# Neighbourhood attention: the channel sums of q and k squares as one fp32 matmul, or as an upper and a lower part in two passes

## The chip, the cores and the metric

The kernel runs on one core of one Trainium2 chip. The metric is device time in microseconds (us) of one execution. The engines of the core are TensorE (PE in the profile, its weight loads PEld), VectorE (DVE), ScalarE (ACT), GpSimd (POOL) and SyncE (SP, which here only issues transfers). Each engine works through its own list of instructions in a fixed order and waits on semaphores for the others.

## The reference, cut to what matters

A two-layer trunk: layer 0 is an mLSTM and Hyena mixer, layer 1 is a 2-D neighbourhood attention; each is followed by a squared-ReLU MLP. The change lies in layer 1, in the normalisation of q and k:

```python
def odd_mixer(hx, hc, w_qkv, qn, kn, rpb, w_out, ctx_out):
    def project(h):
        p = (h @ w_qkv).reshape(b_, l_, 3, NA_HEADS, NA_HD)       # 16 heads of 64 channels
        q = rms_norm(p[:, :, 0], qn) * NA_HD ** -0.5               # x * rsqrt(mean(x*x) + EPS) * gain
        k = rms_norm(p[:, :, 1], kn)
        v = p[:, :, 2]
    ...
```

There are 1024 latent tokens and 256 context tokens, 1024 channels, all in float32.

## The kernel before, in words

Activations lie with channels on the 128 partitions and tokens along the free dimension, in three groups of tokens: two of 512 latent tokens and one of 256 context tokens (`GR`). Products of weights and activations are made from split operands: a float32 value is held as an upper part, rounded to the type fp32r, and a lower part, the remainder in fp32r (`split`, lines 110 to 113: ACT copies, which rounds, and DVE subtracts). A projection (`gemm`, lines 170 to 180) issues three fp32r matmuls for each of 8 blocks of channels: 24 matmuls for one group.

The attention layer goes over 8 pairs of heads. For each pair, `natten_proj` makes q, k and v. It works group by group: two groups of q (q0, q1), three of k (k0, k1, k2) and three of v (v0, v1, v2). Each q or k group goes through `normed`: ACT squares the projection out of PSUM (L900), PE sums the squares over the 64 channels of each head by a matmul with a block matrix of ones, `bd` (L902), ACT takes the mean, the logarithm and the exponential (L904 to L906), and DVE refines the reciprocal root and applies it (L907 to L913). ACT then rounds the result into `Q` or `Kt` (L932, L938) and DVE makes the lower parts (helper line L96). So five calls of `normed` stand in each pair, 40 in all: 32 of 512 tokens and 8 of 256. Both operands of L902 are plain float32; each such matmul shows in the trace as two PE records.

`natten_attn` then treats four column blocks of the grid (`cb`), each for the two heads of the pair (`hh`): scores (PE, L978 and L979), row maximum and bias (DVE, L982 to L986), exponentials (ACT, L989 and L990), division (DVE, L994), transposes of the probabilities (PE, L999 and L1006), copies of them to SBUF (ACT L1001 into tiles of the tag `s2`; DVE L1008), and the product with v (PE, L1014 and L1018). After the last pair the output projection follows.

Nothing in the source fixes the order in which the two functions of neighbouring pairs interleave. A scheduler lays the instructions of each engine out before the run, by priorities and by when it thinks that operands and buffers are free. The attention is written under `pr("na")`, a raised priority of 500; `natten_proj` under `pr("np")`, which has none. Buffers are part of it. PSUM holds three banks for projections (`g`), three for scores and outputs (`f`), one for transposes (`m`) and one for the sums of squares (`n`): `PS3` in line 63. In SBUF, `s2()` and `n2()` are two sets of four buffers of 128x512 each (lines 86 to 90). Before the change, a call of `normed` takes three `n2` buffers (`sq`, which later serves as `v`, then `y` and `r`), and no `s2` buffer; the transposed probabilities of a column block take four `s2` buffers.

Of the kernel before, what the change touches and what calls it, by code (L numbers as in the profile page):

```python
# [9 lines left out]
F32 = mybir.dt.float32  # L10
F32R = mybir.dt.float32r
AF = mybir.ActivationFunctionType
ALU = mybir.AluOpType
# [4 lines left out]
P = 128  # L18
# [9 lines left out]
def kernel(ctx: ExitStack, tc: tile.TileContext, A, out):  # L28
    nc = tc.nc
    V, S, T, G = nc.vector, nc.scalar, nc.tensor, nc.gpsimd  # L30
    cnt = [0]

    base = ctx.enter_context(tc.tile_pool(name="base", bufs=1))
# [5 lines left out]
    def mk(pool, shape, tag, bufs, dt=F32):  # L39
        cnt[0] += 1  # L40
        return pool.tile(shape, dt, tag=tag, bufs=bufs, name=f"{tag}_{cnt[0]}")
# [18 lines left out]
    def pr(k):  # L60
        k = HP.get(k, k)
        return ExitStack() if k is None else tc.high_priority(k)
# [13 lines left out]
    def pt(shape, tag):  # L76
        cnt[0] += 1
        return psp[0].tile(shape, F32, tag=tag, bufs=psp[1][tag], name=f"ps{tag}_{cnt[0]}")
# [7 lines left out]
    def s2(shape=None):  # L86
        return mk(base, shape or [P, 512], "s2", 4)

    def n2(shape=None):
        return mk(base, shape or [P, 512], "n2", 4)  # L90
# [4 lines left out]
    def tt(o, a, b, op, e=None):  # L95
        return (e or V).tensor_tensor(out=o, in0=a, in1=b, op=op)  # L96
# [4 lines left out]
    def sub(o, a, b):  # L101
        return tt(o, a, b, ALU.subtract)

    def mul(o, a, b):
        return tt(o, a, b, ALU.mult)

    def stt(o, a, s, b, op0, op1):
        return V.scalar_tensor_tensor(out=o, in0=a, scalar=s, in1=b, op0=op0, op1=op1)  # L108
# [41 lines left out]
    def wload(at, src, e=None, ks=(0, 8), into=None):  # L150
        with pr(at):
            wp_ = wpool[0]
            raw = mk(wp_, [P, 8, P], "wr", 1)
            r = slice(*ks)
            nc.sync.dma_start(raw[:, r], src)
            if into is None:
                hi = mk(wp_, [P, 8, P], "wh", 2, F32R)
                lo = mk(wp_, [P, 8, P], "wl", 2, F32R)
            else:
                hi, lo = [mk(into[0], [P, 8 * P], t, into[2], F32R).rearrange("p (k c) -> p k c", c=P) for t in into[1]]  # L160
            split(hi[:, r], lo[:, r], raw[:, r], e)
        for f in msteps[:MS]:
            f()
        del msteps[:MS]
        return hi, lo
# [4 lines left out]
    def gemm(w, h, g, n, M=P, ks=range(8), tag="g"):  # L170

        hi, lo = w
        hh, hl = h
        ps = pt([P, 512], tag)
        ks = list(ks)
        for i, k in enumerate(ks):
            T.matmul(ps[:M, :n], hi[:, k, :M], hh[g][:, k, :n], start=(i == 0), stop=False)  # L177
            T.matmul(ps[:M, :n], hi[:, k, :M], hl[g][:, k, :n], start=False, stop=False)  # L178
            T.matmul(ps[:M, :n], lo[:, k, :M], hh[g][:, k, :n], start=False, stop=(i == len(ks) - 1))  # L179
        return ps  # L180
# [697 lines left out]
    KC0 = (0, 8, 24, 32)  # L878

    def natten_consts(pool):  # L880
        bd = mk(pool, [P, P], "bd", 1)
        nc.scalar.dma_start(bd, A["bdones"])
        qk = mk(pool, [P, 2], "qkn", 1)
        nc.scalar.dma_start(qk, A["qkn"])
        gain = mk(pool, [P, 1], "gain", 1)
        stt(gain, qk[:, 0:1], 0.125, qk[:, 1:2], ALU.mult, ALU.mult)
        return bd, gain

    def natten_proj(hp, h, ap_, nl, cst, order=((0, 0), (0, 1), (1, 0), (1, 1), (1, 2), (2, 0), (2, 1), (2, 2))):

        with pr("np"):
            bd, gain = cst

            Q = [mk(nl, [P, LAT], "Q", 4, F32R) for _ in range(2)]
            Ql = [mk(nl, [P, LAT], "Ql", 3, F32R) for _ in range(2)]
            for hh in range(2):
                G.memset(Ql[hh][64 - 64 * hh:128 - 64 * hh].bitcast(F32), 0.0)
            def normed(ps, n, sc):
                sq = n2()
                S.activation(sq[:, :n], ps[:, :n], AF.Square)  # L900
                p2 = pt([P, 512], PN)
                T.matmul(p2[:, :n], bd, sq[:, :n], start=True, stop=True)  # L902
                v, y, r = sq, n2(), n2()
                S.activation(v[:, :n], p2[:, :n], AF.Identity, bias=epsc, scale=1.0 / 64)  # L904
                S.activation(y[:, :n], v[:, :n], AF.Ln)
                S.activation(y[:, :n], y[:, :n], AF.Exp, scale=-0.5)  # L906
                mul(r[:, :n], y[:, :n], y[:, :n])  # L907
                stt(v[:, :n], r[:, :n], -0.5, v[:, :n], ALU.mult, ALU.mult)
                stt(r[:, :n], v[:, :n], 1.5, y[:, :n], ALU.add, ALU.mult)
                if sc is None:  # L910
                    mul(r[:, :n], ps[:, :n], r[:, :n])
                else:
                    stt(r[:, :n], ps[:, :n], sc, r[:, :n], ALU.mult, ALU.mult)  # L913
                return r

            Kt = [mk(ap_, [P, NT], "KK", 4, F32R) for _ in range(2)]
            vT = mk(nl, [P, NT], "vT", 2)
            w = {}
            for j, g in order:
                t0, n = GR[g]  # L920
                if j not in w:
                    w[j] = wload("qkv" if hp else "q0", A["w_qkv"][3 * hp + j], E4 if hp == 0 else None, into=(nl, ("Q", "Q"), 4) if hp == 0 and j == WQ else None)
                ts = slice(t0, t0 + n)
                ps = gemm(w[j], h, g, n)
                if j == 0:
                    r = normed(ps, n, gain)
                    blkd = lambda x: x.rearrange("p (c r q) -> p c r q", c=4, q=16)
                    rv = r.rearrange("p (r c q) -> p c r q", c=4, q=16)
                    for hh in range(2):
                        a = slice(64 * hh, 64 * hh + 64)  # L930
                        for b in (0, 64):
                            S.copy(blkd(Q[hh][b:b + 64, ts]), rv[a])  # L932
                        sub(blkd(Ql[hh][a, ts]), rv[a], blkd(Q[hh][a, ts]).bitcast(F32))
                elif j == 1:
                    r = normed(ps, n, None)
                    for hh in range(2):
                        a, b = slice(64 * hh, 64 * hh + 64), slice(64 - 64 * hh, 128 - 64 * hh)
                        S.copy(Kt[hh][a, ts], r[a, :n])  # L938
                        sub(Kt[hh][b, ts], r[a, :n], Kt[hh][a, ts].bitcast(F32))
                else:  # L940
                    with pr("v0" if hp == 0 else None):
                        S.copy(vT[:, ts], ps[:, :n])
            return Q, Ql, Kt, vT
# [169 lines left out]
    with tc.tile_pool(name="gp", bufs=1, reuse_waits="tile", side="right") as gp:  # L1113
        cst = mlstm_consts(gp)
        with tc.tile_pool(name="ml", bufs=1, reuse_waits="tile") as ml:
# [35 lines left out]
            for d in range(FM[2], 8):  # L1151
                out1(d)
    gkc.close()
    cst = natten_consts(ctx.enter_context(tc.tile_pool(name="cn", bufs=1, side="right")))
    with tc.tile_pool(name="xg", bufs=1, reuse_waits="tile", side="right") as xp:
        xg = [mk(xp, [P, 8, n], f"x{g}", 1) for g, (t0, n) in enumerate(GR)]
# [5 lines left out]
        for g, (t0, n) in enumerate(GR):  # L1162
            for d in range(8):
                hi, lo = [x[:, 2 * (d % 4):2 * (d % 4) + 2] for x in w2[d // 4]]
# [53 lines left out]
    with tc.tile_pool(name="xg1", bufs=1, reuse_waits="tile", side="right") as xp:  # L1218
# [3 lines left out]
        hi, lo = wload("ow2", A["w_o"][:, :, 7].rearrange("d p c -> p d c"), E1)  # L1222
# [145 lines left out]
```

## Time and profile before

| | |
|---|---|
| median of 3 runs | 3346.32 us (3345.22 to 3348.22) |
| the profiled execution: time, span | 3341.84 us, 3340.1 us |
| PE busy in the span | 3232.4 us (97%) |
| DVE, ACT, POOL busy | 2056.8 (62%), 1200.4 (36%), 96.5 us (3%) |
| mean granted TensorE clock | 0.991 |
| first and last matmul with `bd` (L902) start | 1916.9 and 2482.1 us |

Busy times are summed from records, and matmul records overlap their neighbours, so the step from one matmul's start to the next says more than a record's length. "idle before, releaser" in a row names what ended an engine's wait. The lines that carry the argument are shown in the prediction.

### The profile page before, as it was taken

Reading aid. Unit: us, or ns where it says so; the run is one execution under the profiler, and the core shown is the slowest. Engines: PE = TensorE matmul, PEld = TensorE weight load, DVE = VectorE, ACT = ScalarE, POOL = GpSimd, SP = SyncE. Lnnn points to the kernel's source line nnn. Section 1 sums busy time; section 2 is a strip of 40 time slices with the busy share of each in tenths; the row PEclk is TensorE's granted clock in tenths of the full one; section 3 lists DMA queues with packets and bytes.
Section 4 is the critical chain, followed back from the end, with each engine's and each line's share of the span. In section 5 each row is a group of like instructions: output and inputs, shape, how many; then the busy total and the mean of one; then the engine's idle time right before and its main releaser. Section 6 shows DMA issues by size and latency. Waiting matters only on the chain.

```text
span 3340.1 us, 45203 instructions
## 1 busy us (share of the span) xinstructions
PE 3232.4 (97%) x18044; PEld 2637.5 (79%) x18044; DVE 2056.8 (62%) x3790; ACT 1200.4 (36%) x2539; POOL 96.5 (3%) x160
## 2 busy tenths in 40 slices
PE   7799999999999999999999999999999999999999
PEld 4678887778877888888888777777777788888887
DVE  4958997556684444544445877666666754455454
ACT  5742221343442212111121576666664422121111
POOL 0000000000000000000000011111110000000000
PEclk9899999999999999999999999999999999999999
DMA  6432224776522212121111221222234111111111
GB/s 208 163 110 67 81 73 146 231 241 208 189 97 95 70 57 89 57 89 64 51 45 32 79 69 59 70 64 70 67 96 144 65 62 46 49 51 47 48 45 70
DMA packets 140876, 306.11 MB, mean 92 GB/s; under 512 B 12497, under 2 KB 74057, under 8 KB 139258
## 3 DMA queue, kind: packets, MB, share of 16 engines
q1 hardware_dynamic: 131018, 266.60, 24.5%
q0 software_dynamic: 6464, 28.84, 2.8%
q10 hardware_dynamic: 3184, 7.78, 0.7%
q8 instruction: 142, 2.33, 0.3%
q14 instruction: 68, 0.56, 0.1%
HBM read 255.93 MB, written 43.05 MB: 90 GB/s over the span
## 4 chain that ended last, share of the span: by engine, by line
PE 77%; DVE 8%; DMA 3%; ACT 2%; issue 1%; SPq 0%; ACTq 0%; DVEq 0%
PE psg L177 13%; PE psg L178 13%; PE psg L179 13%; PE psf L313 8%; PE psf L312 8%; PE psf L314 8%; DMA wm<-in_w_mod 3%; PE psf L1014 2%; PE psm L999 1%; DVE b L96 1%; PE psf L978 1%; PE psf L979 1%; DVE n L108 1%; DVE q L96 1%; PE psf L1018 1%; PE psm L218 1%
## 5 line engine op out<-in xcount | busy, mean ns | idle before, releaser
L177 PE MATMUL psg<-h,wh 128*128 128x512 f32 (+1 forms) x2728 | 1014.8, 372 | 13.5 <-ACT h L289 7.1
L179 PE MATMUL psg<-h,wl 128*128 128x512 f32 (+1 forms) x2728 | 1003.9, 368 | 5.7 <-DVE wl L113 5.4
L178 PE MATMUL psg<-h,wh 128*128 128x512 f32 (+1 forms) x2728 | 1007.9, 370 | 1.0 <-DVE h L108 0.9
L177 PEld LDWEIGHTS psg<-h,wh 128*128 128x128 f32 x2728 | 516.5, 189 | 109.4 <-issue 17.3
L179 PEld LDWEIGHTS psg<-h,wl 128*128 128x128 f32 x2728 | 516.2, 189 | 93.4 <-DVE wl L113 10.6
L178 PEld LDWEIGHTS psg<-h,wh 128*128 128x128 f32 x2728 | 516.3, 189 | 91.7 <-issue 14.2
L108 DVE SCALAR_TENSOR_TENSOR x<-psf,modT,x 128x512 f32<-128x512 f32 (+1 forms) x512 | 347.1, 683 | 218.8 <-PE psf L314 218.7
L313 PE MATMUL psf<-al,w2h 128*128 128x512 f32 (+1 forms) x1280 | 471.6, 369 | 0.6 <-DVE al L113 0.6
L314 PE MATMUL psf<-ah,w2l 128*128 128x512 f32 (+1 forms) x1280 | 470.9, 368 | 0.0
L312 PE MATMUL psf<-ah,w2h 128*128 128x512 f32 (+1 forms) x1280 | 468.6, 369 | 0.1
L112 ACT CAST w2h<-w2r 128x1024 fp32r<-128x1024 f32 x64 | 67.3, 1051 | 765.9 <-PE psf L313 595.9
L113 DVE TENSOR_TENSOR wl<-wr,wh 128x1024 fp32r<-128x1024 f32 (+2 forms) x144 | 172.9, 1200 | 213.3 <-ACT wh L112 212.7
L312 PEld LDWEIGHTS psf<-ah,w2h 128*128 128x128 f32 x1280 | 240.4, 188 | 44.4 <-ACT ah L112 2.6
L313 PEld LDWEIGHTS psf<-al,w2h 128*128 128x128 f32 x1280 | 241.2, 189 | 43.3 <-DVE al L113 2.3
L314 PEld LDWEIGHTS psf<-ah,w2l 128*128 128x128 f32 x1280 | 241.2, 188 | 40.4 <-issue 0.5
L112 ACT CAST wh<-wr 128x1024 fp32r<-128x1024 f32 (+2 forms) x144 | 148.4, 1031 | 249.2 <-PE psg L178 207.6
L108 DVE SCALAR_TENSOR_TENSOR rr<-psg,rr 128x512 f32<-128x512 f32 x160 | 101.3, 633 | 176.6 <-ACT rr L301 176.6
L113 DVE TENSOR_TENSOR w2l<-w2r,w2h 128x1024 fp32r<-128x1024 f32 x64 | 78.2, 1222 | 151.6 <-ACT w2h L112 149.9
L301 ACT ACTIVATE rr<-psg 128x512 f32<-128x512 f32 x160 | 88.0, 550 | 194.7 <-PE psg L179 193.3
L113 DVE TENSOR_TENSOR al<-rr,ah 128x512 fp32r<-128x512 f32 x160 | 101.8, 636 | 84.1 <-ACT ah L112 84.1
L112 ACT CAST ah<-rr 128x512 fp32r<-128x512 f32 x160 | 92.4, 578 | 170.0 <-DVE rr L108 170.0
L108 DVE SCALAR_TENSOR_TENSOR h<-psf,modT,h 128x512 f32<-128x512 f32 x128 | 94.2, 747 | 44.2 <-PE psf L314 44.2
(286 smaller groups left out, 4046.2 us busy)
## 6 DMA issues: line engine op xcount, KB each, us to landing
wm<-in_w_mod SPq DMA_DIRECT2D x96, 512.0 KB
wr<-in_w SPq DMA_DIRECT2D x64, 512.0 KB
w2r<-in_w SPq DMA_DIRECT2D x64, 512.0 KB
big<-d SPq DMA_DIRECT2D x39, 640.0 KB
TM<-in_rpbT POOLq DMA_DIRECT2D x64, 384.0 KB, 3.4
wr<-in_w_in SPq DMA_DIRECT2D x29, 512.0 KB
wr<-in_w_qkv SPq DMA_DIRECT2D x24, 512.0 KB
d<-b SPq DMA_DIRECT2D x8, 1280.0 KB
```

The costliest lines, as they stand in the source:

```text
L96: return (e or V).tensor_tensor(out=o, in0=a, in1=b, op=op)
L108: return V.scalar_tensor_tensor(out=o, in0=a, scalar=s, in1=b, op0=op0, op1=op1)
L112: S.copy(hi, x)
L113: (e or V).tensor_tensor(out=lo, in0=x, in1=hi.bitcast(F32), op=ALU.subtract)
L177: T.matmul(ps[:M, :n], hi[:, k, :M], hh[g][:, k, :n], start=(i == 0), stop=False)
L178: T.matmul(ps[:M, :n], hi[:, k, :M], hl[g][:, k, :n], start=False, stop=False)
L179: T.matmul(ps[:M, :n], lo[:, k, :M], hh[g][:, k, :n], start=False, stop=(i == len(ks) - 1))
L301: S.activation(r[:, :n], ps[:, :n], AF.Relu)
L312: T.matmul(ps[:, :n], w2h[:, d], ah[g], start=(i == 0), stop=False)
L313: T.matmul(ps[:, :n], w2h[:, d], al[g], start=False, stop=False)
L314: T.matmul(ps[:, :n], w2l[:, d], ah[g], start=False, stop=(i == 1))
L1014: T.matmul(po[64 * hh:64 * hh + 64, rb], Vw[:, rb + j, 64 * hh:64 * hh + 64], pT[hh][0][rb][:, j], start=(j == 0), stop=False)
```

## The change

`bd` is kept as fp32r; it is loaded into a plain tile first and copied by ACT. The squares are split into an upper part (`hi`, a fourth `n2` buffer) and a lower part (`lo`, an `s2` buffer), and L902 becomes two fp32r matmuls into the same PSUM bank.

```diff
     def natten_consts(pool):
-        bd = mk(pool, [P, P], "bd", 1)
-        nc.scalar.dma_start(bd, A["bdones"])
+        bd, raw = mk(pool, [P, P], "bd", 1, F32R), s2([P, P])
+        nc.scalar.dma_start(raw, A["bdones"])
+        S.copy(bd, raw)
...
             def normed(ps, n, sc):
-                sq = n2()
+                sq, hi = n2(), mk(base, [P, 512], "n2", 4, F32R)
                 S.activation(sq[:, :n], ps[:, :n], AF.Square)
+                S.copy(hi[:, :n], sq[:, :n])
+                lo = mk(base, [P, 512], "s2", 4, F32R)
+                tt(lo[:, :n], sq[:, :n], hi[:, :n].bitcast(F32), ALU.subtract)
                 p2 = pt([P, 512], PN)
-                T.matmul(p2[:, :n], bd, sq[:, :n], start=True, stop=True)
+                T.matmul(p2[:, :n], bd, hi[:, :n], start=True, stop=False)
+                T.matmul(p2[:, :n], bd, lo[:, :n], start=False, stop=True)
                 v, y, r = sq, n2(), n2()
```

The scheduler also lays out the whole attention layer anew. Lines of the changed kernel behind L902 are five higher: L904 becomes L909, L999 becomes L1004, and so on; the copy to `hi` is L902 there, and the two matmuls are L906 (upper part) and L907 (lower part).

The first place is PE, in the attention of the second pair of heads. Before, the matmul with `bd` for a group of the next pair (`psn`) stands between scores (`psf`), transposes (`psm`) and projections (`psg`):

```order
L954 MATMUL psm_18103<-ident,vs_18101 128x128 x4
L978 MATMUL psf_18167<-KK_17530,Q_17524 128x384
L979 MATMUL psf_18167<-KK_17530,Ql_17526 128x384
L902 MATMUL psn_18441<-n_3270_18439,bd_8340 128x512
L999 MATMUL psm_18138<-ident,pe_18119 128x128 x3
L178 MATMUL psg_18464<-h_1651_8778,wh_18460 128x512
L179 MATMUL psg_18464<-h_1650_8777,wl_18461 128x512
L177 MATMUL psg_18464<-h_1650_8777,wh_18460 128x512
```

Now the transposes of the last column block follow on one another with no projection between them:

```order
L984 MATMUL psf_18371<-KK_17582,Ql_17578 128x384
L1004 MATMUL psm_18342<-ident,pe_18323 128x128 x3
L1004 MATMUL psm_18348<-ident,pe_18329 128x128 x3
L1019 MATMUL psf_18408<-s_3265_18346,Vw_18312 64x128
L1011 MATMUL psm_18354<-ident,pe_18323 128x128 x2
L1011 MATMUL psm_18354<-ident,pe_18329 128x128 x2
L1004 MATMUL psm_18389<-ident,pe_18370 128x128 x3
L1004 MATMUL psm_18395<-ident,pe_18376 128x128 x3
```

and the lower part for q0 of the next pair stands directly behind the last of these transposes:

```order
L1023 MATMUL psf_18408<-pc_18359,Vc_17922 64x128
L1011 MATMUL psm_18401<-ident,pe_18370 128x128 x2
L1011 MATMUL psm_18401<-ident,pe_18376 128x128 x2
L907 MATMUL psn_18478<-s_3298_18476,bd_8340 128x512
L1023 MATMUL psf_18408<-pc_18406,Vc_17922 64x128
```

Its upper part (L906 into the same `psn_18478`) stands 149 rows further up, in the middle of the attention. Between the two, projections of two more groups are found, q1 and k0; the last of their matmuls stands 50 rows ahead of L907. With q0 they fill the three `g` banks.

The second place is ACT, at the start of the second of the five calls. Before, the work of the attention (`pe`, `s`, `o`, `Vw`) stands between the steps of a call:

```order
L904 ACTIVATE n_3270_18439<-psn_18441,epsc 128x512
L905 ACTIVATE n_3272_18443<-n_3270_18439 128x512
L906 ACTIVATE n_3272_18443<-n_3272_18443 128x512
L1001 COPY s_3216_18189<-psm_18185 128x384
L1001 COPY s_3218_18195<-psm_18191 128x384
L900 ACTIVATE n_3278_18489<-psg_18464 128x512
L989 ACTIVATE pe_18246,st_18240<-pe_18246,st_18240 128x384
L1192 COPY o_18225<-psf_18204 128x256
L990 ACTIVATE pe_18246,st_18240<-psf_18239,st_18240 128x256
```

Now the calls of one pair stand behind one another, and the first step of a call (L909) behind the four roundings (L937) of the call ahead of it:

```order
L909 ACTIVATE n_3296_18472<-psn_18478,epsc 128x512
L910 ACTIVATE n_3300_18481<-n_3296_18472 128x512
L911 ACTIVATE n_3300_18481<-n_3300_18481 128x512
L901 ACTIVATE n_3303_18521<-psg_18496 128x512
L1197 COPY o_18429<-psf_18408 128x256
L902 CAST n_3304_18522<-n_3303_18521 128x512
L937 CAST Q_18432<-n_3301_18482 64x512 x2
L937 CAST Q_18433<-n_3301_18482 64x512 x2
L909 ACTIVATE n_3303_18521<-psn_18527,epsc 128x512
```

The pattern repeats for pairs 2 to 7. SP's transfers keep their order; on POOL two neighbours change places in each pair. Outside the attention layer only the load and copy of `bd` move, near 895 us.

## The prediction

> **What bounds the kernel now.** I read the table of engines first, then the table of stretches over the attention layer, cut where the scores of a new pair of heads begin (1947.5, 2015.3, 2094.1 us).
>
> ```profile
> PE 3232.4 (97%) x18044; PEld 2637.5 (79%) x18044; DVE 2056.8 (62%) x3790; ACT 1200.4 (36%) x2539; POOL 96.5 (3%) x160
> ```
> ```profile
> core 0: us, PE busy (x) PEld busy (x) DVE busy (x) ACT busy (x) POOL busy (x), PEclk, DMA share, GB/s
> 1947.50:2015.30 67.80, 63.67 (x444) 49.22 (x444) 50.24 (x121) 48.81 (x123) 10.32 (x16) 1.00 0.23 71
> 2015.30:2094.10 78.80, 78.40 (x528) 61.78 (x528) 54.47 (x123) 51.59 (x129) 11.91 (x18) 1.00 0.22 68
> ```
>
> One pair takes 78.8 us, and PE works 78.4 of them. DVE has 54.5 us of work in it and ACT 51.6, so neither limits, provided that the projection of the next pair always lies beside the attention of this one. The first pair (67.8 us) already leaves PE idle for 4.1 us.
>
> **What the change saves on PE.** The chain of work shows what the two fp32 passes hold PE for, and the timeline of PE what an fp32r matmul holds it for (step from start to start):
>
> ```profile
> 2069.49 0.86 PE psn L902 x2
> ```
> ```profile
> 1949.46 0.39 PE L177 MATMUL psg<-h,wh 128*128 128x512 f32 x1
> 1949.69 0.39 PE L178 MATMUL psg<-h,wh 128*128 128x512 f32 x1
> ...
> 2496.74 0.28 PE L177 MATMUL psg<-h,wh 128*128 128x256 f32 x1
> 2496.86 0.28 PE L178 MATMUL psg<-h,wh 128*128 128x256 f32 x1
> ```
>
> A call of 512 tokens holds PE for 0.86 us, and afterwards for 2 x 0.23 (1949.69 - 1949.46) = 0.46: 0.40 saved. For 256 tokens half of 0.86 is 0.43, and 2 x 0.12 = 0.24 stay: 0.19. Over 32 and 8 calls this is 12.8 + 1.5 = 14.3 us, 4 x 0.40 + 0.19 = 1.8 per pair.
>
> **What it adds.** Each call gains a rounding on ACT and a subtraction on DVE ahead of its matmul. The MLP's split has both in the same shape:
>
> ```profile
> L113 DVE TENSOR_TENSOR al<-rr,ah 128x512 fp32r<-128x512 f32 x160 | 101.8, 636 | 84.1 <-ACT ah L112 84.1
> L112 ACT CAST ah<-rr 128x512 fp32r<-128x512 f32 x160 | 92.4, 578 | 170.0 <-DVE rr L108 170.0
> ```
>
> That is 4.5 x 0.58 = 2.6 us of ACT and 4.5 x 0.64 = 2.9 us of DVE per pair. By busy time alone the 78.8 us would cover both. But the order of the instructions is new, and two things in it take the cover away. The lower part lives in an `s2` buffer; all four of these go to the attention's probabilities first, so the lower part of q0 waits until the attention of the running pair is through. Meanwhile q0, q1 and k0 hold the three `g` banks, and PE has no projection to put between the last column blocks. And as a call now takes all four `n2` buffers, the calls follow one another, on ACT literally: the first step of q1 stands behind the roundings of q0's result.
>
> **Term 1, the projection as a chain.** Durations from the groups of one pair (2039.2 to 2118.1 us), shapes kept apart:
>
> ```profile
> L904 ACT ACTIVATE n<-psn,epsc 128x512 f32<-128x512 f32 x4 | 2.8, 690 | 1.3 <-PE psn L902 1.3
> L905 ACT ACTIVATE n<-n 128x512 f32<-128x512 f32 x4 | 2.6, 638 | 0.1
> L906 ACT ACTIVATE n<-n 128x512 f32<-128x512 f32 x4 | 2.5, 632 | 0.1
> L96 DVE TENSOR_TENSOR n<-n 128x512 f32<-128x512 f32 x4 | 2.8, 689 | 0.0
> L108 DVE SCALAR_TENSOR_TENSOR n<-n,n 128x512 f32<-128x512 f32 x8 | 5.5, 692 | 0.3
> L108 DVE SCALAR_TENSOR_TENSOR n<-psg,gain,n 128x512 f32<-128x512 f32 x2 | 1.5, 748 | 0.0
> L932 ACT CAST Q<-n 64x512 fp32r<-64x512 f32 x8 | 4.9, 618 | 0.1
> L938 ACT CAST KK<-n 64x512 fp32r<-64x512 f32 x4 | 2.5, 612 | 0.0
> L112 ACT CAST wh<-wr 128x1024 fp32r<-128x1024 f32 x3 | 3.1, 1047 | 3.5 <-PE psg L178 3.5
> L108 DVE SCALAR_TENSOR_TENSOR n<-n,n 128x256 f32<-128x256 f32 x2 | 0.9, 426 | 0.1
> ```
>
> From the first ACT step of q0 to that of q1: 0.69 + 0.64 + 0.63 on ACT, 0.69 + 2 x 0.69 + 0.75 on DVE, 4 x 0.62 on ACT: 7.25 us. q1 to k0 the same. k0 to k1 has two roundings instead of four, and the rounding of a weight block (1.05) inside: 7.0. k1 to k2: 5.95. k2, at 256 tokens 0.426 / 0.692 of that, and the lower part of k: 4.1. Sum 31.6, and some twenty handovers of 0.03 us: 32.2 us from the lower part of q0 to the next pair's scores, which need all five. PE has in this time, by the new order, 62 projection matmuls of 512 tokens (62 x 0.23 = 14.3) and 24 of 256 (2.9), the second half of an output (1.7) and nine passes of `bd` (1.9): 20.8. So PE stands idle for 11.4 us per pair. No row shows such a chain without cover; the bounds are 8 us (if extra steps found their place while the matmuls run) and 15 us (if each handover via PE costs another 0.5).
>
> **Term 2, the end of the attention without cover.** The first pair before has a piece of just this order. Transposes of a column block's two heads begin:
>
> ```profile
> 1955.94 0.49 PE L999 MATMUL psm<-ident,pe 128*128 128x128 f32 x3
> ...
> 1961.58 0.52 PE L999 MATMUL psm<-ident,pe 128*128 128x128 f32 x3
> ...
> 1970.07 0.49 PE L999 MATMUL psm<-ident,pe 128*128 128x128 f32 x3
> ...
> 1985.32 0.52 PE L999 MATMUL psm<-ident,pe 128*128 128x128 f32 x3
> ...
> 1990.32 0.52 PE L999 MATMUL psm<-ident,pe 128*128 128x128 f32 x3 [0.46 <-DVE pe L994]
> ...
> 1992.70 0.66 PE L1006 MATMUL psm<-ident,pe 128*128 128x128 f32 x4
> ...
> 1998.66 0.44 PE L978 MATMUL psf<-KK,Q 128*128 128x384 f32 x1 [1.27 <-ACT pe L990]
> ...
> 2000.85 0.52 PE L999 MATMUL psm<-ident,pe 128*128 128x128 f32 x3 [0.57 <-DVE pe L994]
> ```
>
> From 1990.32 to 2000.85 the rows of PE are those of the new order, and 10.5 us pass; the wait of 1.27 is for a score bank that the exponentials hold. From one head's transposes to the other's, 5.0 us (1985.32 to 1990.32); from these to the end of the last transposes 2.8 (1992.70 + 0.4). The uncovered end thus takes 10.5 + 5.0 + 2.8 = 18.3 us. PE's work of attention per pair is 78.4 less 144 x 0.23 + 48 x 0.12 for projections and 3.9 for L902, 35.6 us, 8.9 per column block; by the counts of rows the end holds 1.15 of one, 10.2. Idle: 8.1 us; bounds 5 and 10. The earlier blocks keep somewhat fewer projections between their steps: 1 us more.
>
> **The sum per pair.** PE's work 78.4 - 1.8 = 76.6, plus 11.4 + 8.1 + 1.0 idle: 97.1, against 78.8: +18.3. Six pairs (the second to the seventh) go so: +110 us.
>
> The first pair has nearly no projection from its second block on. From its scores (1947.5) to the first transposes 8.4 us, to the second head's 5.6, three times from second head to first (8.5 at 1961.58, 10.5 at 1990.32; I take 9.6), twice 5.0, the end 7.8, the chain 32.2: 92.8 against 67.8: +25. Its own projection, ahead of its scores, becomes such a chain as well: L904 of q0 starts at 1918.4, the scores at 1947.5, 29.1 us later. The chain needs 32.2 and two copies of v (0.9) that stand in it, and starts 0.6 later: +4.6. The last pair has other work beside it, in the old order: 0.
>
> The load of `bd`: ACT waits in its place before, too, and longer than a load and a copy:
>
> ```profile
> 905.72 0.62 ACT L112 CAST h<-big 128x512 fp32r<-128x512 f32 x1 [3.67 <-DVE big L108]
> ```
>
> Cost 0 to 1 us, taken as 0, while that idle time lasts. Total: 110 + 25 + 5 = +140 us on the profiled execution (3341.84 us), which lies 4.5 us under the median: 3482, and **3486 us** for the median.
>
> **Rivals.** *The saving decides.* If the lower parts came in time and the calls overlapped as before, PE would gain its 14.3 us: 3332 us. The 97% of PE speak for it. It turns where the idle time added per pair is under 1.8 us; the order, in which one call's first step stands behind the last step of the one ahead, puts 11. Chance 0.04.
>
> *Only the chain.* If the attention's end held no more idle time than before, because without `normed` beside it DVE is freer: 6 x (11.4 - 1.8) + 11 (the chain behind the first pair) + 5 = 74 us, 3420. Against it speaks that DVE's extra work between 1990 and 2001 us was only some of the delay. Chance 0.12.
>
> *The clock falls.* Where PE is half idle, the granted clock (the column behind POOL) can drop:
>
> ```profile
> 1998.00:2000.00 2.00, 1.34 (x4) 0.59 (x4) 2.00 (x7) 1.10 (x5) 0.59 (x1) 1.00 0.21 66
> 2000.00:2002.00 2.00, 0.79 (x4) 0.31 (x3) 1.92 (x6) 1.66 (x4) 0.90 (x2) 1.00 0.18 43
> ...
> 2498.00:2500.00 2.00, 0.94 (x4) 0.40 (x3) 1.09 (x1) 1.46 (x3) 0.00 (x0) 1.00 0.32 40
> 2500.00:2502.00 2.00, 1.15 (x7) 0.92 (x7) 0.00 (x0) 0.61 (x2) 0.61 (x1) 0.87 0.83 253
> 2504.00:2506.00 2.00, 2.00 (x9) 1.59 (x9) 0.00 (x0) 0.36 (x1) 0.00 (x0) 0.50 1.06 409
> ```
> ```profile
> 2501.47 0.90 PE L999 MATMUL psm<-ident,pe 128*128 128x128 f32 x3 [0.68 <-ACT Vw L956]
> ```
>
> After 2.1 busy us in 4 it fell to half at 2502 us, and after as much it stayed at 2002. At half, three transposes take 0.90 instead of 0.52. On the path of the end lie six such steps and 1.2 us of scores, in the chain four lower passes: 6 x 0.38 + 1.2 + 4 x 0.24 = 4.4 us per pair, 31 over seven: 3517. Chance 0.16. [...]
>
> **How the numbers follow.** The forecast has 0.68. Its own bounds are 6 x (5 + 8 + 0 - 1.8) + 20 + 3 = 90 and 6 x (10 + 15 + 2 - 1.8) + 32 + 7 = 190 us at the extremes of all terms together; two thirds of the way to each, 3453 and 3520, is its likely range. With the clock's case above and half of "only the chain" below, I give 3430 to 3535. About 0.2% (7 us) is what a measurement of this kernel can tell. Slower: 0.94, the three slow cases less 0.02 for smaller stalls than any of them that just eat the saving; faster 0.04; same 0.02.
>
> **What would show it.** In the new profile a pair should last some 97 us, PE busy about 80% there, and DVE and ACT hardly more than before. L904's successor on ACT should wait for DVE or PE, and the subtraction of `lo` should begin only when L994's successor is done. PE should wait for ACT or DVE at the matmuls with `bd` and at the first scores of a pair. If pairs last under 80 us, the order did not bind as I read it; if matmuls show twice their length, the clock is in it.

## The result, and the profile after

The changed kernel takes 3505.57 us (median of six runs, 3505.08 to 3513.44) against 3345.77 us of the kernel before on the same chip: a ratio of 1.0481, interval 1.0470 to 1.0492, or 160 us slower. The forecast was 3486. The profiled execution took 3505.44 us, with a span of 3503.7 and a mean granted clock of 0.968 (before: 0.991).

The table of engines of the changed kernel:

```profile
PE 3284.4 (94%) x18044; PEld 2681.2 (77%) x18044; DVE 2078.7 (59%) x3830; ACT 1226.3 (35%) x2580; POOL 97.9 (3%) x160
```

The span grew by 163.6 us. PE's busy time grew by 52.0 of them, with no more matmuls than before, and its idle time by 111.6. DVE and ACT have only 22 and 26 us more to do. So PE waits more, and some of its matmuls last longer.

The table of stretches, cut at the first scores of the first, second and third pair of heads (length, then busy time of PE, PEld, DVE, ACT and POOL, the granted clock, DMA):

```profile
1956.90:2055.10 98.20, 76.17 (x448) 58.37 (x447) 55.84 (x126) 51.62 (x127) 10.77 (x16) 0.84 0.16 49
2055.10:2154.40 99.30, 83.69 (x525) 66.13 (x525) 56.01 (x127) 54.78 (x134) 12.12 (x18) 0.91 0.18 54
```

The second pair takes 99.3 us where it took 77.4 (the five after it took 78.9 each before), and the first one 98.2 where it took 67.8. In 99.3 us PE is busy for 83.7 and idle for 15.6. The clock column is 0.91; before it was 1.00 in each of the first seven pairs.

The waits of PE within the attention layer, up to the start of the last pair (1900 to 2660 us; us in total, times, longest), say where the idle time is. Line numbers after L904 are five higher than before; L906 and L907 are the matmuls of the upper and the lower part:

```profile
PE psn L906 <- ACT n L902: 64.4, 19, 5.4
PE psm L1004 <- DVE pe L999: 28.8, 22, 1.9
PE psm L1004 <- ACT s L1006: 14.3, 24, 0.7
```

The first row is the projection as a chain: PE stands before the sums of squares until ACT has made the upper part. The other two are the end of the attention, where transposes wait for divisions, and for the copy that frees the PSUM bank. Before, the same waits up to the start of the last pair (1900 to 2500 us) came to 0.4 and to 4.3 us:

```profile
PE psm L999 <- ACT s L1001: 2.4, 8, 0.7
PE psm L999 <- DVE pe L994: 1.9, 7, 0.6
PE psn L902 <- ACT n L900: 0.4, 2, 0.3
```

How the chain starts is in DVE's timeline, and how it goes on in ACT's (the step that reads the sums, once for each of the five calls, between the second and the third pair's scores):

```profile
2119.36 0.69 DVE L96 TENSOR_TENSOR s<-n,n 128x512 fp32r<-128x512 f32 x1 [3.13 <-PE psf L1019]
```
```profile
2120.94 0.69 ACT L909 ACTIVATE n<-psn,epsc 128x512 f32<-128x512 f32 x1 [2.11 <-PE psn L907]
2128.49 0.69 ACT L909 ACTIVATE n<-psn,epsc 128x512 f32<-128x512 f32 x1
2136.05 0.69 ACT L909 ACTIVATE n<-psn,epsc 128x512 f32<-128x512 f32 x1
2143.96 0.69 ACT L909 ACTIVATE n<-psn,epsc 128x512 f32<-128x512 f32 x1 [0.30 <-PE psn L907]
2150.20 0.47 ACT L909 ACTIVATE n<-psn,epsc 128x256 f32<-128x256 f32 x1
```

The lower part of q0 (`s<-n,n`) is made only when the attention's product L1019 has given an `s2` buffer back, at 2119.36, at the very end of the running pair. From there the calls follow at 7.55, 7.56, 7.91 and 6.24 us, and the scores come at 2154.5, another 4.3 us later. Within the chain ACT makes the next call's upper part only when a DVE step of the call ahead (L108) has given an `n2` buffer back, and this is the wait of PE in the first row above:

```profile
2125.21 0.62 ACT L902 CAST n<-n 128x512 fp32r<-128x512 f32 x1 [1.52 <-DVE n L108]
```

Last, the clock, in stretches of the same pair, with the transposes beside them in PE's timeline:

```profile
2108.00:2110.00 2.00, 0.81 (x4) 0.30 (x2) 1.74 (x5) 0.78 (x3) 0.62 (x2) 1.00 0.45 179
2110.00:2112.00 2.00, 0.52 (x3) 0.31 (x3) 1.34 (x6) 1.35 (x5) 1.04 (x2) 1.00 0.24 34
2112.00:2114.00 2.00, 1.51 (x9) 1.08 (x9) 0.15 (x1) 1.73 (x6) 0.00 (x0) 0.90 0.47 163
```
```profile
2114.00:2116.00 2.00, 0.47 (x3) 0.12 (x2) 1.55 (x5) 0.00 (x0) 0.00 (x0) 0.50 0.00 0
2118.00:2120.40 2.40, 2.40 (x18) 1.88 (x17) 0.69 (x1) 0.48 (x1) 0.00 (x0) 0.50 0.00 0
2120.40:2124.00 3.60, 2.24 (x29) 1.69 (x27) 1.68 (x3) 2.70 (x5) 0.01 (x1) 1.00 0.00 0
2121.00:2126.00 5.00, 1.86 (x27) 1.62 (x28) 3.31 (x6) 3.31 (x7) 0.69 (x1) 1.00 0.08 26
2127.00:2130.00 3.00, 3.00 (x9) 2.34 (x8) 1.04 (x2) 2.89 (x6) 0.00 (x0) 0.54 0.02 5
```
```profile
2111.03 0.52 PE L1004 MATMUL psm<-ident,pe 128*128 128x128 f32 x3 [1.57 <-DVE pe L999]
...
2115.91 0.87 PE L1004 MATMUL psm<-ident,pe 128*128 128x128 f32 x3 [1.53 <-DVE pe L999]
2117.36 0.90 PE L1004 MATMUL psm<-ident,pe 128*128 128x128 f32 x3 [0.57 <-ACT s L1006]
```

The clock (the column behind POOL) falls from 1.00 to 0.50 late in the stretch from 2112 to 2114, at the end of the attention, is back at 1.00 from 2120.4, and halves again after 2127, within the chain (and a third time from 2140.9 to 2147.7). Three transposes then last 0.87 to 0.90 us in place of 0.52.

### The profile page after: what moved, and what is told of

The parts are those of the page before. It is cut to its first block, busy times and chain, and to the rows that moved or that the text cites. A ratio compares the mean times of both kernels' runs of the same rounds, so it can differ in the third digit from the quotient of the medians.

```text
span 3503.7 us, 45363 instructions
## 1 busy us (share of the span) xinstructions
PE 3284.4 (94%) x18044; PEld 2681.2 (77%) x18044; DVE 2078.7 (59%) x3830; ACT 1226.3 (35%) x2580; POOL 97.9 (3%) x160
## 4 chain that ended last, share of the span: by engine, by line
PE 71%; DVE 11%; ACT 5%; DMA 4%; issue 1%; SPq 0%; ACTq 0%; DVEq 0%
PE psg L177 12%; PE psg L179 12%; PE psg L178 11%; PE psf L313 7%; PE psf L312 7%; PE psf L314 7%; DVE n L108 2%; DMA wm<-in_w_mod 2%; PE psf L1019 2%; PE psm L1004 2%; DVE b L96 1%; PE psf L983 1%; ACT Q L937 1%; PE psm L1011 1%; DVE n L96 1%
## 5 line engine op out<-in xcount | busy, mean ns | idle before, releaser
L177 PE MATMUL psg<-h,wh 128*128 128x512 f32 (+1 forms) x2728 | 1015.6, 373 | 13.6 <-ACT h L289 7.0
L177 PEld LDWEIGHTS psg<-h,wh 128*128 128x128 f32 x2728 | 522.0, 191 | 109.5 <-issue 15.0
L178 PEld LDWEIGHTS psg<-h,wh 128*128 128x128 f32 x2728 | 521.7, 191 | 90.0 <-issue 8.5
L108 DVE SCALAR_TENSOR_TENSOR x<-psf,modT,x 128x512 f32<-128x512 f32 (+1 forms) x512 | 347.2, 683 | 218.7 <-PE psf L314 218.5
L108 DVE SCALAR_TENSOR_TENSOR rr<-psg,rr 128x512 f32<-128x512 f32 x160 | 101.4, 634 | 177.5 <-ACT rr L301 177.5
L108 DVE SCALAR_TENSOR_TENSOR h<-psf,modT,h 128x512 f32<-128x512 f32 x128 | 94.3, 748 | 44.1 <-PE psf L314 44.1
```

## The experiments

Twelve kernels were run. Edits are against the changed kernel where nothing else is said. This table gathers what their profiles show of the attention layer: from the first matmul with `bd` to the first scores, from there to the third pair's scores, and the mean of the five pairs from the third to the seventh (us). Since the layer itself begins at times that differ by up to 18 us between kernels (the first matmul with `bd` starts between 1910.3 and 1928.0 us), lengths are compared and not positions.

| kernel | median of runs | ratio to before (95%) | bd to scores | first two pairs | each later pair |
|---|---|---|---|---|---|
| before | 3345.8 to 3348.0 | 1 | 30.7 | 145.2 | 78.9 |
| changed | 3505.57 | 1.0481 (1.0470 to 1.0492) | 36.8 | 197.5 | 99.8 |
| sq_in_s2 | 3454.93 | 1.0322 (1.0305 to 1.0338) | 41.1 | 182.0 | 93.8 |
| hi_only | 3332.56 | 0.9950 (0.9936 to 0.9964) | 30.9 | 146.4 | 76.6 |
| lo_in_n2 | 3353.02 | 1.0016 (1.0007 to 1.0024) | 38.3 | 147.4 | 77.9 |
| prio_s2 | 3501.33 | 1.0458 (1.0444 to 1.0472) | 38.7 | 198.4 | 98.9 |
| no_chain | 3507.79 | 1.0476 (1.0462 to 1.0490) | 38.2 | 192.7 | 99.0 |
| no_chain_n2 | 3352.18 | 1.0011 (1.0003 to 1.0020) | 40.5 | 156.3 | 77.1 |
| prio_n2 | 3354.33 | 1.0023 (1.0014 to 1.0032) | 38.8 | 152.5 | 77.8 |
| n2_four | 3352.12 | 1.0010 (1.0001 to 1.0019) | 40.1 | 155.8 | 76.5 |
| n2_three | 3352.41 | 1.0012 (1.0004 to 1.0021) | 39.2 | 152.8 | 77.1 |
| n2_two | 3327.25 | 0.9943 (0.9930 to 0.9957) | 31.3 | 136.8 | 77.0 |
| before_two | 3344.07 | 0.9992 (0.9983 to 1.0001) | 31.3 | 142.2 | 78.7 |
| s2_two | 3490.81 | 1.0429 (1.0415 to 1.0443) | 31.5 | 197.7 | 97.6 |

**lo_in_n2: the lower part in another set of buffers.** Everything else stays, the number of matmuls, roundings and subtractions too.

```diff
-                lo = mk(base, [P, 512], "s2", 4, F32R)
+                lo = mk(base, [P, 512], "n2", 4, F32R)
```

> The changed kernel with one word changed: the lower part of the squares takes its buffer from the tag n2, which the attention does not use, and no longer from s2. All of the change's instructions stay: 40 more roundings on ACT, 40 more subtractions on DVE, two passes of bd. Theory A (the s2 buffer makes q0's lower part wait for the end of the running attention, and this takes the cover from everything behind it): the projections stand beside the attention again, a pair lasts 77 to 80 us and not 100, in all 3335 us (3328 to 3355). Theory B (the added work of ACT and DVE, or the two passes themselves, cost the time): it stays slow, 3480 to 3510 us. Theory C (four or more n2 buffers per call chain the five calls to one another, and that chain costs it): five n2 buffers per call now, so no faster than the changed kernel, 3480 to 3560 us.

3353.02 us: one word takes back 152 of the 160 us. The bulk of the loss is the `s2` buffer, not the work that the split adds. PE does the same matmuls in 3226.9 busy us at a mean granted clock of 0.988, in place of 3284.4 at 0.968, so the slower clock had made PE's records up to 57.5 us longer. But the saving on PE did not show either; the experiments from no_chain_n2 on look for it.

**sq_in_s2: the kernel before, with the buffer alone.**

```diff
-                sq = n2()
+                sq = s2()
```

> The kernel before with one word changed: the square in normed takes an s2 buffer where it took an n2 buffer. Nothing is split, bd and the squares stay plain float32, no instruction is added. Theory A: the square of q0 waits for the end of the running attention, which loses its cover (8 us of idle PE per pair, 1 us earlier on, some 1.5 us for a fallen clock); the chain of calls is shorter than in the changed kernel, since a call takes two n2 buffers and one s2 buffer and the next can begin while it runs (3 us of idle PE): +13 us per pair and +25 for the first, some 3450 us (3400 to 3490). Theory B: no added work, so no loss: 3340 to 3352 us. Theory C: fewer n2 buffers per call, so no loss or a little gain: 3335 to 3350 us.

3454.93 us. With no split at all and the two fp32 passes kept, taking `normed`'s first buffer from `s2` costs 108 us. One of its pairs in the table of stretches:

```profile
2133.37:2227.29 93.92, 85.12 (x524) 64.92 (x525) 53.01 (x122) 52.08 (x129) 11.51 (x18) 0.93 0.18 57
```

The pattern is that of the changed kernel: PE idle for 8.8 us, and the clock at 0.93.

**hi_only: one pass.** The kernel before, with the squares written by ACT as fp32r and summed in a single pass; the lower part of the squares is left out. `v`, `y` and `r` are three further `n2` buffers.

```diff
-                sq = n2()
-                S.activation(sq[:, :n], ps[:, :n], AF.Square)
+                hi = mk(base, [P, 512], "n2", 4, F32R)
+                S.activation(hi[:, :n], ps[:, :n], AF.Square)
...
-                T.matmul(p2[:, :n], bd, sq[:, :n], start=True, stop=True)
-                v, y, r = sq, n2(), n2()
+                T.matmul(p2[:, :n], bd, hi[:, :n], start=True, stop=True)
+                v, y, r = n2(), n2(), n2()
```

> Only one half of the change: the square is written by ACT as fp32r straight away and summed in one pass of bd; the lower part is left out of the sums, and with it the rounding, the subtraction, the s2 buffer and the second pass. It tells what PE's time at bd is worth where nothing waits for it. Per call 0.86 - 0.23 = 0.63 us less for 512 tokens and 0.43 - 0.12 = 0.31 for 256: 32 x 0.63 + 8 x 0.31 = 22.6 us. Theory A: PE is the bound wherever the attention covers the projections, so all of it comes back: 3323 us (3318 to 3330). If the fp32 passes lay in time that PE would have waited anyway: 3340 to 3348 us.

3332.56 us, 14 faster than before where 22.6 were expected, and between the two ranges. A later pair is 2.3 us shorter, where a single fp32r pass in place of the two fp32 ones should give 4 x 0.63 + 0.31 = 2.8. The saving on PE is real; the first two pairs, 1.2 us longer than before, take a little of it back, and what takes the rest was not looked for.

**prio_s2: the order by priority.** Was the lower part late because the attention has the higher priority? Here squares, split, matmuls and the requests for their buffers got a higher one than the attention's.

```diff
+                with tc.high_priority(600):
+                    ... the squares, the split, the two matmuls and their buffers, as they were
```

> The changed kernel with the steps of normed up to the two matmuls (square, rounding, lower part, sums) under a raised priority of 600, above the attention's 500; the buffers stay as in the changed kernel. It tells why the lower part gets its s2 buffer so late. If the attention takes the four buffers first because its priority is higher (as the prediction has it): the lower part now comes first, the cover returns, 3335 to 3380 us. If the buffers of a tag go to their users in the order of the program text, in which the attention of a pair stands ahead of the projection of the next, priority doesn't help: 3480 to 3520 us, with the lower part of q0 still behind the last transposes.

3501.33 us: no relief. The lower part of q0 still waits for the attention's product, which is L1020 here:

```profile
2121.78 0.69 DVE L96 TENSOR_TENSOR s<-n,n 128x512 fp32r<-128x512 f32 x1 [3.13 <-PE psf L1020]
```

So the raised priority doesn't let the lower part have an `s2` buffer ahead of the attention that stands before it in the program's text. The prediction's words that the buffers "go to the attention's probabilities first" hold, and not by priority; that the order of the text decides is the other of the two explanations set down before the run, and fits it.

**no_chain: two `n2` buffers per call.** The prediction blamed the chain of calls on the four `n2` buffers that each call takes. Here the Newton step works in the PSUM bank of the sums and in the squares' own buffer, with as many operations, so that only `sq` and `hi` are `n2` buffers. The lower part stays in `s2`.

```diff
-                v, y, r = sq, n2(), n2()
+                v, y = p2, sq
...
-                mul(r[:, :n], y[:, :n], y[:, :n])
-                stt(v[:, :n], r[:, :n], -0.5, v[:, :n], ALU.mult, ALU.mult)
-                stt(r[:, :n], v[:, :n], 1.5, y[:, :n], ALU.add, ALU.mult)
+                stt(v[:, :n], y[:, :n], -0.5, v[:, :n], ALU.mult, ALU.mult)
+                mul(v[:, :n], v[:, :n], y[:, :n])
+                stt(y[:, :n], v[:, :n], 1.5, y[:, :n], ALU.add, ALU.mult)
+                r = y
```

> As the changed kernel, the lower part still in an s2 buffer, but a call needs only two n2 buffers (the Newton step works in the PSUM bank of the sums and in the squares' own buffer, same number of operations), so that calls no longer follow one another through the fourth n2 buffer. Theory A (two costs add: the bare end of the attention, and the chain of calls behind it): the order now has 24 projection matmuls between two calls of the chain, which cover it; the end of the attention stays bare. Per pair 8 to 11 us less than the 99.7 of the changed kernel, in all 3425 us (3405 to 3455), still 70 to 100 above before. Theory B (the wait for s2 alone makes the loss, the fourth n2 buffer adds nothing): 3480 to 3505.

3507.79 us, no faster: theory A missed by some 80 us, and theory B's range by 3. The waits of PE in this kernel show a new one of the old size:

```profile
PE psn L906 <- DVE n L108: 64.8, 24, 5.4
```

There is a single PSUM bank for the sums, and it was now held through the whole Newton step; the next call's L906 waits for its last reader, a DVE step. One chain was exchanged for another, so this run doesn't tell what the `n2` buffers cost. s2_two, below, does.

**no_chain_n2: the same with the lower part in `n2`.** As no_chain, and in addition the edit of lo_in_n2: three `n2` buffers per call.

> Both causes taken away: the lower part in an n2 buffer, and the Newton step in PSUM, so that a call takes three n2 buffers as before the change. Theory A (what ate the saving in the kernel with lower parts in n2 was the five buffers per call: first scores 7.9 us later, first pair 4.2 longer): both come back, and PE's saving of 14.3 us shows: 3333 us (3327 to 3340), faster than before. Theory B (the saving is smaller than 14.3 on PE, or the split's two extra steps per call cost elsewhere, the one psn bank now being held some 4 us longer per call): 3343 to 3360, no faster than before.

3352.18 us: the saving still doesn't show. A later pair is 1.8 us shorter than before, as forecast, but the first calls take 40.5 us in place of 30.7 and the first two pairs 156.3 in place of 145.2.

**prio_n2: lo_in_n2 with the priority of prio_s2.**

> Lower part in n2 (five n2 buffers per call), with a scheduling priority on squares, split and the sums' matmuls, so that their place in the order comes earlier. Theory A (buffers, not the order's priorities, hold the first pair back): the first scores still come 5 to 8 us later than before, the 2.2 us of idle time in every third pair go: 3343 us (3337 to 3352). Theory B (the order's priorities are what ate the saving): 3333 us (3327 to 3337).

3354.33 us, outside both expectations and no better than lo_in_n2. The order by priority isn't what ate the saving.

**n2_four, n2_three, n2_two: a series over the buffers of a call.** All of them do the changed kernel's computation, with the PSUM bank given back early. n2_four has its lower part in `n2` and a Newton step in two buffers instead of three. n2_three writes both parts into the call's own destination, which is of the right type and is overwritten with the results later, and keeps the old Newton step. n2_two does both:

```diff
-            def normed(ps, n, sc):
-                sq, hi = n2(), mk(base, [P, 512], "n2", 4, F32R)
+            def normed(ps, n, sc, hi, lo):
+                sq = n2()
...
-                lo = mk(base, [P, 512], "s2", 4, F32R)
...
-                v, y, r = sq, n2(), n2()
+                v, y = sq, n2()
...
-                mul(r[:, :n], y[:, :n], y[:, :n])
-                stt(v[:, :n], r[:, :n], -0.5, v[:, :n], ALU.mult, ALU.mult)
-                stt(r[:, :n], v[:, :n], 1.5, y[:, :n], ALU.add, ALU.mult)
+                stt(v[:, :n], y[:, :n], -0.5, v[:, :n], ALU.mult, ALU.mult)
+                mul(v[:, :n], v[:, :n], y[:, :n])
+                stt(v[:, :n], v[:, :n], 1.5, y[:, :n], ALU.add, ALU.mult)
+                r = v
...
-                    r = normed(ps, n, gain)
+                    r = normed(ps, n, gain, Q[0][:, ts], Q[1][:, ts])
...
-                        r = normed(ps, n, None)
+                        r = normed(ps, n, None, Kt[0][:, ts], Kt[1][:, ts])
```

> A series over the number of n2 buffers that a call takes from the pool's four, the computation otherwise the changed kernel's. Here four: lower part in n2, the Newton step without its third buffer (same number of operations, early release of the PSUM bank). Theory A (calls held apart by the pool's buffers ate the saving; five per call: first scores 7.9 us late, first pair 4.2 longer): half of that comes back, 3343 us (3337 to 3348). Theory B (the split's own steps, 0.6 us on ACT and 0.7 on DVE per call, lengthen the five calls ahead of the first scores, whatever the buffers): first scores still 7 us or more late, 3350 to 3356.

> Three n2 buffers per call, as before the change: the upper and the lower part are written into the call's own destination (two Q or two KK tiles of the same type, overwritten with the results afterwards), the Newton step as in the changed kernel. Theory A: first scores at most 4 us later than before, first pair at most 2 us longer, per pair 1.8 less: 3336 us (3331 to 3341), faster than before. Theory B: first scores 7 us or more late, 3346 to 3354, no faster.

> Two n2 buffers per call: parts in the call's own destination and the Newton step without its third buffer, so that two calls can always overlap. Theory A: first scores within 2 us of before, first pair no longer than before: 3333 us (3328 to 3338). Theory B: as with three buffers, 3346 to 3354.

3352.12, 3352.41 and 3327.25 us. It isn't a slope but a step: five, four and three buffers give the same time, and only two let the saving through. n2_three needs as many buffers as the kernel before, and still its first calls take 39.2 us in place of 30.7: 8.5 us over five calls, 1.7 per call, about a rounding of 0.62, a subtraction of 0.69 and their handovers. So where one call follows the other, as it does ahead of the first scores and in the first pair, which have little else for PE, the split's two steps lie on the path (theory B). With two buffers per call the next call works beside the one that runs, and they don't (theory A). ACT's first two squares of the layer, in n2_three and then in n2_two, show it: the second call begins 8.05 us after the first in the one and 5.40 in the other.

```profile
1922.02 0.60 ACT L901 ACTIVATE n<-psg 128x512 f32<-128x512 f32 x1 [0.67 <-DVE h L108]
1930.07 0.61 ACT L901 ACTIVATE n<-psg 128x512 f32<-128x512 f32 x1
```
```profile
1917.67 0.60 ACT L901 ACTIVATE n<-psg 128x512 f32<-128x512 f32 x1 [0.67 <-DVE h L108]
1923.07 0.59 ACT L901 ACTIVATE n<-psg 128x512 f32<-128x512 f32 x1
```

The first two pairs of n2_three, and the first pair of n2_two, in the tables of stretches of the two kernels:

```profile
1963.14:2115.97 152.83, 144.31 (x963) 114.46 (x963) 109.87 (x251) 103.98 (x261) 22.20 (x34) 0.96 0.22 66
```
```profile
1950.94:2011.18 60.24, 60.15 (x422) 48.22 (x420) 51.64 (x124) 49.46 (x126) 9.77 (x15) 1.00 0.25 78
```

PE is idle for 8.5 us in the one and for 0.1 in the other. n2_two is the fastest kernel of this study that computes what the reference asks for.

**before_two: what of n2_two is the change's.** The kernel before, unsplit, with n2_two's Newton step.

```diff
-                v, y, r = sq, n2(), n2()
+                v, y = sq, n2()
...  (the Newton step as in n2_two)
```

> The kernel before, its squares unsplit, with the Newton step in two n2 buffers per call instead of three. It gives the kernel against which the split in two buffers per call (3327 us) has to be measured. Theory A (the split saves PE its 14.3 us when buffers are equal; what two buffers bring beside it is the shorter first pair): 3341 us (3336 to 3346), the first pair some 7 us shorter, the later pairs at 78.6 as before. Theory B (the saving on PE is nearly nothing and two buffers bring all): 3325 to 3332.

3344.07 us, some 3 less than before, with an interval that touches 1. Against it n2_two is 16.8 us faster by the medians (17.8 when each is held against its own runs of before); the intervals of the two ratios are far apart. So with equal buffers the split is worth some 17 us; the intervals are too wide to tell this from the 14.3 us of the prediction. The rows of two pairs each, of the kernel before and of n2_two, show where:

```profile
2092.76:2250.66 157.90, 157.06 (x1049) 123.31 (x1049) 108.03 (x243) 103.27 (x259) 23.81 (x36) 1.00 0.22 67
```
```profile
2087.69:2241.18 153.49, 153.10 (x1050) 123.20 (x1049) 111.33 (x253) 107.80 (x268) 24.26 (x36) 1.00 0.22 69
```

PE's work in two pairs falls from 157.06 to 153.10, 1.98 per pair where 1.8 was forecast. DVE gains 1.65 and ACT 2.3 us per pair, which cost nothing there.

**s2_two: the wait for `s2` alone.** As n2_two, and the edit is against it, but with the lower part in an `s2` buffer: two `n2` buffers per call, PSUM given back early, nothing but `s2` scarce.

```diff
-            def normed(ps, n, sc, hi, lo):
+            def normed(ps, n, sc, hi):
...
+                lo = mk(base, [P, 512], "s2", 4, F32R)[:, :n]
...  (both calls of normed lose their last argument)
```

> The changed kernel's wait for s2 alone, with nothing else between the calls: lower part in s2, upper part in the call's own destination, two n2 buffers per call, the PSUM bank released early. Theory A (bare end of the attention and chained calls are two costs): the end stays bare, some 10 us per pair, the chain of calls is gone: 86 to 90 us per pair, 3405 us (3385 to 3430). Theory B (once the calls begin after the attention, the scores need all five whatever the buffers; ACT and DVE steps of five calls, laid one after another, are the chain): 96 us per pair or more, 3475 to 3505.

3490.81 us, 15 less than the changed kernel: theory B. Its second pair, and in it the stretch from the first lower part's matmul to the next scores, with the waits of PE from 1900 to 2660 us:

```profile
2051.50:2150.81 99.31, 85.99 (x525) 67.27 (x525) 55.94 (x127) 54.00 (x134) 12.21 (x18) 0.91 0.18 54
2115.50:2150.81 35.31, 27.65 (x128) 21.36 (x126) 22.37 (x36) 22.12 (x40) 0.69 (x1) 0.85 0.06 19
```
```profile
PE psn L906 <- ACT KK L903: 20.5, 10, 2.9
PE psm L1005 <- DVE pe L1000: 16.9, 10, 1.9
PE psn L907 <- DVE s L96: 15.5, 14, 1.4
PE psm L1005 <- ACT s L1007: 15.4, 26, 0.7
```

The chain still takes 35 us. ACT and DVE are each busy for some 22 of them, PE for 27.7; none is full, but each call goes to and fro between them, and PE waits in turn for the rounding (L903), for the subtraction and, at the next projection, for its bank (L177 behind DVE's L108, 7.3 us in 10 waits). What makes the loss is that the five calls can begin only when the attention of the running pair has ended. The two `n2` buffers that the changed kernel takes beyond these, with its longer chain through them, add about 2.2 us per pair (99.8 against 97.6).

## Why the prediction was right, point by point

- **What the split saves on PE (14.3 us, 1.8 per pair).** Right on PE, as closely as it was measured: 1.98 per pair between the kernel before and n2_two, 13.3 us of PE's busy time over the whole kernel (3232.4 to 3219.1), and 17 us of the time between before_two and n2_two. In the changed kernel itself nothing of it shows.
- **The lower part waits for an `s2` buffer.** Right, and shown: lo_in_n2 takes it away and gets 152 us back, sq_in_s2 puts it into the kernel before and loses 108. That the attention doesn't come first by its priority was not in the prediction; prio_s2 showed it.
- **Term 1, the chain.** 32.2 us were forecast from the lower part of q0 to the scores, and 34.1 measured (2120.4 to 2154.5): steps of 7.55, 7.56, 7.91 and 6.24 for 7.25, 7.25, 7.0 and 5.95. The 0.03 us per handover is what lies between two ACT steps of a call before (L904 from 2060.20 for 0.70 us, L905 at 2060.93); the further 0.5 us per handover via PE, in the upper bound, was an estimate that no run isolates. The length was right; the cause was only half right. I let the calls follow one another because each takes all four `n2` buffers, and in the changed kernel ACT does wait for DVE's last steps of the call ahead. But s2_two takes two buffers and its chain is as long, so what holds the calls apart there lies elsewhere, in the waits shown with it; no run took these away.
- **Term 2 and the earlier blocks.** 97.1 less 32.2 leaves 64.9 us for the rest of the pair; 65.3 were measured (2055.1 to 2120.4).
- **The sum per pair.** 97.1 forecast, 99.3 measured, but made up otherwise. (The 78.8 us that it starts from were cut 1.3 us late: the third pair's first scores stand at 2092.76. The later pairs took 78.9, so the base holds.) I had PE working for 76.6 us and idle for 20.5; it was busy for 83.7 and idle for 15.6. The 7 us more of busy time fit the clock, 0.91 in this pair: lo_in_n2, with the same matmuls and a granted clock of 0.988 (1.00 from 2102.88 to 2260.19, behind its second pair), has 75.4 busy us in its second pair of 75.5. Part of them may lie in time in which PE would have stood idle anyway. That the two errors, 7.1 us too little work and 4.9 us too much idle time, left the sum so close is in part luck. Over the whole kernel six pairs gave 127 us where 110 were forecast, the first pair 30 for 25, and the start 6.1 for 4.6.
- **The clock as a rival.** I held "the forecast" and "the clock falls" apart, at 0.68 and 0.16. In the run both came true at once: the clock halved in every one of these pairs, in both of the places that its sum counts, the attention's end and the chain (in the second pair to 0.50 at 2113.58 and at 2127.24 us). With it I had put 3517; 3505.6 came. In the prediction two stretches of 4 us with 2.1 busy us each, one with a fall behind it and one without, looked alike; in the 3.41 us up to 2003.11, where the clock stayed, PE was busy for 2.12, and in the 3.41 us up to 2501.46, where it fell, for 1.51 (last section). No run kept PE's clock up while leaving the waits, so how much of the 160 us is the clock's is not isolated; the 57.5 us of busy time between the changed kernel and lo_in_n2 are an upper bound, since much of it lies beside waits.
- **The first pair (92.8) and the calls ahead of it (+4.6).** 98.2 and +6.1 (36.8 against 30.7). Both forecasts were too low; the clock was 0.84 in the first pair.
- **The load of `bd`, 0 to 1 us.** ACT waits for it once, for 0.9 us, and copies for 0.3; no wait of PE on it shows.
- **Rival "the saving decides" (3332).** Its figure was reached in this study, but only by n2_two, with other buffers. My condition for it, that the idle time added per pair stays under 1.8 us, was too narrow: lo_in_n2 meets it in the later pairs (77.9 against 78.9) and still gives 3353, since the calls ahead of the first scores (+7.6) and the first pairs (+2.2) take the saving back. The terms for the start, which I had only added to the slow case, decide there.

## What to carry to other kernels

A change that adds a scratch buffer should be priced first by who else uses that set of buffers and who stands ahead in the program's text: here the one word "s2" cost 152 us, and the arithmetic that was changed was worth some 17. A saving on the engine that bounds the kernel shows only if the steps that the change adds elsewhere find cover everywhere, also at the start of a stage, where there is little other work; counting the buffers that one call needs, so that two calls fit into the set, is what let it through. Writing intermediate values into the tile that will hold the result costs no buffer at all.

## What the runs showed of the hardware

In the pair shown, the clock fell to 0.50 at 2113.58, at 2127.24 and at 2140.89 us. The first fall came after 4 us (2108 to 2112) in which PE had worked for 1.33, with 1.57 us as the longest wait; the second after 5 us (2121 to 2126) with 1.86, and 2.69 us as the longest. The second one lasted 3.41 us (2127.24 to 2130.65), and the three falls lie 13.66 and 13.65 us apart, four times as much; within the trace of the kernel before and within that of the changed kernel, all changes of the clock lie a whole number of such steps of 3.41 us apart. These are such steps, the first two in the kernel before (at 2003.11 the clock stayed at 1.00, at 2501.46 it fell to 0.50), the others in the changed kernel (it fell to 0.50 at the end of each):

```profile
1999.70:2003.11 3.41, 2.12 (x11) 1.00 (x10) 2.22 (x6) 2.73 (x7) 1.20 (x2) 1.00 0.35 115
2498.05:2501.46 3.41, 1.51 (x8) 0.82 (x7) 1.09 (x1) 2.02 (x4) 0.53 (x1) 1.00 0.51 108
```
```profile
2110.17:2113.58 3.41, 1.61 (x10) 0.99 (x11) 1.17 (x6) 2.85 (x9) 0.87 (x2) 1.00 0.42 115
2123.83:2127.24 3.41, 1.36 (x6) 1.13 (x7) 3.23 (x5) 1.88 (x4) 0.69 (x1) 1.00 0.13 41
2137.48:2140.89 3.41, 0.00 (x0) 0.00 (x0) 2.49 (x3) 1.87 (x3) 0.00 (x0) 1.00 0.09 10
```

In these five the busy share of the step goes with the change: 62% kept the clock, 44, 47, 40 and 0% lost it. Two other steps of the changed kernel are less far apart and lie the other way round: with 1.96 busy us, 57%, the clock fell (2000.95 to 2004.36), and with 1.74, 51%, it stayed (2021.43 to 2024.84). No run changed the share alone, so what sets the moment is not shown.

At a clock of 0.50 a projection matmul of 512 tokens starts 0.43 us after the last one (2127.92 to 2128.35), in place of 0.23 at 1.00 (2126.22 to 2126.45), and three transposes take 0.87 to 0.90 us in place of 0.52:

```profile
2127.92 0.63 PE L179 MATMUL psg<-h,wl 128*128 128x512 f32 x1
2128.35 0.63 PE L177 MATMUL psg<-h,wh 128*128 128x512 f32 x1
```

In this pair time so goes into the many short waits of PE and, beside them, into longer matmuls; no run shows how much of the second comes from the first.
